# Attention's second pass, block by block: one two-bank score tile, one exponential, and both groups' value products side by side

## The chip, the cores and the metric

The kernel runs on one core of a Trainium2 chip. The metric is the device time of one execution in microseconds, the median of several. Before the change it is 3320.48 us, the median of 3 runs (3320.19 to 3322.39).

## The reference, cut to what matters

The kernel computes two networks one after the other: a first block of two layers (an mLSTM mixer, then sliding-window attention, each with a feed-forward part) and a second block of two layers, each of which sums attention, gated linear attention (GLA) and a gated unit (SGU). The change touches the three attentions: that of the sliding window, and one in each layer of the second block. The second block's, over 512 latent and 256 context tokens, with 8 query heads in 2 key/value groups of 4:

```python
def attend(q, k, v):
    s = jnp.einsum('btgrd,blgd->bgrtl', q, k, preferred_element_type=jnp.float32) * (ATTN_HEAD_DIM ** -0.5)
    p = jax.nn.softmax(s, axis=-1)
    return jnp.einsum('bgrtl,blgd->btgrd', p.astype(v.dtype), v)
```

In the first of these layers the context tokens attend as well, among themselves. The sliding window has 16 query heads in 4 groups; a chunk of 128 latent queries sees the 256 context keys and the latent keys at most 128 positions away, and the softmax has one more term, a sink:

```python
s_lat = jnp.where(valid, s_lat, -jnp.inf)
m = jnp.maximum(jnp.maximum(jnp.max(s_lat, -1), jnp.max(s_ctx, -1)), sink_g)
p_lat = jnp.exp(s_lat - m[..., None])
p_ctx = jnp.exp(s_ctx - m[..., None])
den = jnp.sum(p_lat, -1) + jnp.sum(p_ctx, -1) + jnp.exp(sink_g - m)
o = jnp.einsum("bhgqk,bkhd->bqhgd", p_lat, vb) + jnp.einsum("bhgqc,bchd->bqhgd", p_ctx, cv)
return o / jnp.moveaxis(den, 3, 1)[..., None]
```

## The kernel before, in words

Large products take every operand as a high and a low part and sum three matmuls (high by high, high by low, low by high). Their results go to PSUM tiles named "acc" (two banks of 512 float32 values a partition, `acc()` at line 351), in some stages to more banks. A weight tile is loaded ("raw"), its high part is made on ScalarE ("whi") and its low part on VectorE or GpSimd ("wlo").

An attention has two passes over the keys, both on chunks of 128 queries. First the projections give keys and queries token by token; `stack_k` (line 1003) and `stack_q` (line 992) split them and transpose them on TensorE (against "k_ident", line 298) into a PSUM tile "st", from which ScalarE and VectorE copy the pieces into the operands "kh", "kl", "q", "q2" (in the sliding window the high keys lie in tiles that the trace calls "uhc" and "ulc").

The first pass (`stats`, line 1029) puts the scores with queries on the partitions into tiles "s" (3 banks), takes the extreme of each row on VectorE and the sum of exponentials on ScalarE. `stats_end` (line 1070) turns both into the logarithm of the softmax's denominator, transposes it (again a tile "st") and stores it by DMA as two more rows of "q2". So the second pass needs no further normalisation.

The second pass (`attend`, line 1111) goes over the blocks of 128 keys, and within a block over the two groups. For each group it puts the scores of four heads, keys on the partitions, into one bank (two matmuls of 512 columns, a third for a masked block), takes the exponential on ScalarE into "pT" and multiplies with the values "vt", adding into "o" (one bank). Group 0 writes partitions 0 to 63 of "o" and group 1 partitions 64 to 127. This product is in plain float32, and the machine runs it as two instructions of 512 columns. The score tiles are the two banks "st"; in later chunks, and for the sliding window's second pair of groups, they alternate with the three banks "s" (`banks`).

In the sliding window (`swa`, line 1140) there are two pairs of groups and four chunks, so eight calls of `attend`, with 4, 5, 5 and 4 key blocks for the four chunks: 36 blocks. Beside each call the statistics of the next chunk and, in the first four, the projections of the second pair are written. The first pair's results go to DRAM ("yd") and come back at the end, the second pair's are split at once. In the second block (`b_attn`, line 1270) the first layer has six chunks (four with 6 blocks, two of context with 2): 28 blocks, and the second has four chunks of 6: 24 blocks. After the attention `fill()` writes the projections for GLA and gates, which have nothing to do with the attention.

PSUM in these stages: acc 2 banks, st 2, s 3, o 1, which makes all eight.

The order on each engine isn't the written order alone. A planner in the language's tile layer walks all instructions with its own estimate of durations, gives each engine the earliest written instruction that its estimate has ready, and writes that order down; tiles with the same name share their buffers, and it adds the waits. The chip then runs each engine's list in that order. This is why matmuls of `fill()` stand between those of `attend` in the trace.

Of the kernel before, what the change touches and what calls it, by code (L numbers as in the profile page):

```python
# [239 lines left out]
class Net:  # L240
# [751 lines left out]
    def stack_q(self, ph, pc, x, q, q2):  # L992

        hl = self.t(ph, [P, 4, 2, 64], "qhl", F32R, bufs=2)
        self.act(hl[:, :, 0, :], x, scale=-0.125)
        self.stt(hl[:, :, 1, :], x, -0.125, hl[:, :, 0, :].bitcast(F32), MULT, SUB)
        pt = self.t(pc, [P, 4, P], "st", bufs=2)
        for r in range(4):
            self.tr(pt[:, r, :], hl[:, r].bitcast(F32).rearrange("p a d -> p (a d)"))
        self.act(q, pt)  # L1000
        self.nc.vector.tensor_copy(q2, pt[0:64])

    def stack_k(self, ph, pc, x, g, his, los):

        hl = self.t(ph, [P, 3, g, 64], "khl", F32R, bufs=1)
        hd = hl[:, 0:2].rearrange("p a g d -> p (a g d)").rearrange("p (g a d) -> p g a d", a=2, d=64)
        self.act(hd, x.unsqueeze(2).to_broadcast([P, g, 2, 64]))
        self.tt(hl[:, 2], x, hd[:, :, 0].bitcast(F32), SUB)
        for o in range(0, g, 2):
            pt = self.t(pc, [P, 4, P], "st", bufs=2)  # L1010
            for r in range(2):
                self.tr(pt[:, r, :], hd[:, o + r].bitcast(F32).rearrange("p a d -> p (a d)"))
            self.tr(pt[:, 2, :], hl[:, 2, o:o + 2].bitcast(F32).rearrange("p g d -> p (g d)"))
            for r in range(2):
                self.nc.vector.tensor_copy(his[o + r], pt[:, r])
                self.act(los[o + r], pt[64 * r:64 * r + 64, 2])
# [53 lines left out]
    def stats_end(self, ph, pc, parts):  # L1070
# [31 lines left out]
        self.split(hv[:, :, :, 0], hv[:, :, :, 1], d)  # L1102
        pt = self.t(pc, [P, P], "st", bufs=2)
        self.tr(pt, hl.bitcast(F32))
# [5 lines left out]

    def attend(self, ph, pc, q, q2, kh, kl, blocks, vs, masks={}, banks=None):


        po = self.t(pc, [P, 4, P], "o", bufs=1)
        for b in blocks:
            w = slice(b * P, b * P + P)
            for g in range(2):
                tag, n = next(banks) if banks else ("st", 2)
                ps = self.t(pc, [P, 4, P], tag, bufs=n)
                self.mm(ps, kh[g][:, w], q[:, 4 * g:4 * g + 4], stop=False)  # L1120
                self.mm(ps, kl[g][0:66, w], q2[0:66, 4 * g:4 * g + 4], start=False, stop=b not in masks)
                if b in masks:
                    self.mm(ps, self.identb, masks[b].unsqueeze(1).to_broadcast([P, 4, P]), start=False)
                pT = self.t(ph, [P, 4, P], "pT", bufs=4)
                self.act(pT, ps, AF.Exp, scale=-1.0)
                self.mm(po[64 * g:64 * g + 64], vs(b, g), pT, start=b == blocks[0], stop=b == blocks[-1])
        return po

# [11 lines left out]
    def swa(self, u, yd):  # L1140
# [10 lines left out]
        with self.pool("sw") as ph, self.pool("sws", side="right") as pg, self.pool("swp", space=PSUM) as pc:  # L1151
# [42 lines left out]
            qs, wq, y = {}, {}, {}  # L1194
            banks = itertools.cycle([("st", 2), ("st", 2), ("s", 3)])

# [21 lines left out]
            def attend(gp, c):  # L1218
# [6 lines left out]
                if c < 3:  # L1225
                    masks[1 + hi] = mb[:, 0]
                po = self.attend(ph, pc, *qs[gp, c], *keys(gp), [0, 1] + list(range(2 + lo, 2 + hi)),
                                 lambda b, g: vt[:, b, 2 * gp + g, :], masks, banks if gp else None)
                if gp == 0:
                    o = self.scr().rearrange("p (r t) -> p r t", r=4)  # L1230
                    self.act(o, po)
                    nc.sync.dma_start(out=yd[:, :, cs], in_=o)
                else:
                    if not y:
                        y.update(self.new_u("l"))
                    self.split(y["l"][0][:, 4:8, cs], y["l"][1][:, 4:8, cs], po)

# [6 lines left out]
            for n in range(8):  # L1244
# [3 lines left out]
                for g in range(2 if n < 4 else 0):  # L1248
                    project(1, g, n)
            for c in range(4):  # L1250
                x = self.scr()
# [18 lines left out]
    def b_attn(self, u, l, yd, fill):  # L1270
# [5 lines left out]
        with self.pool("at") as ph, self.pool("ats", side="right") as pg, self.pool("atp", space=PSUM) as pc:  # L1276
# [79 lines left out]
            half = len(qch) // 2  # L1356
            banks = itertools.cycle([("st", 2), ("st", 2), ("s", 3)])
            stats(qch[:half])
            for j, c in enumerate(qch):
                if j == 0:  # L1360
                    stats(qch[half:])
                t = slice(c * P, (c + 1) * P)
                po = self.attend(ph, pc, *qs[c], kh, kl, list(range(6 if c < 4 else 2)), lambda b, g: vt[:, b, g, :],
                                 banks=banks if j >= 2 else None)
                self.stt(yf[:, :, t], po, 0.5, yf[:, :, t], MULT, MULT)
                nc.sync.dma_start(out=yd[:, :, t], in_=yf[:, :, t])
            fill()
# [389 lines left out]
    def run(self):  # L1757
        nc = self.nc
        self.nw, self.nsc, self.nth, self.bg = 4, 5, 0, None
        with self.pool("cp") as self.cp, self.pool("up") as self.up, self.pool("sc") as self.sc, \  # L1760
# [217 lines left out]
```

## Time and profile before

| what | value |
|---|---|
| median of 3 runs | 3320.48 us |
| profiled execution, its own time | 3330.69 us |
| profiled execution, span | 3328.9 us |
| instructions | 51048, of them 19813 matmuls |
| VectorE busy | 1775.5 us (53%) |
| ScalarE busy | 1313.9 us (39%) |
| GpSimd busy | 1000.4 us (30%) |
| DMA, mean | 108 GB/s |

The profile is of one execution, and its span begins with the first instruction and ends with the last. An engine is busy while it has an instruction in work. Matmuls overlap one another: a row's duration is longer than the distance to the next one's start, so their durations can't simply be added; distances between starts are what the engine's time is made of. PEld is the loading of weights, which runs beside the matmuls. A merged row of the timeline ("x2", "x4") is so many instructions of one form that follow one another, from the first start to the last end. In square brackets stands how long the engine was idle before it, and what ended that.

### The profile page before, as it was taken

Reading aid. Unit: us, or ns where it says so; the run is one execution under the profiler, and the core shown is the slowest. Engines: PE = TensorE matmul, PEld = TensorE weight load, DVE = VectorE, ACT = ScalarE, POOL = GpSimd, SP = SyncE. Lnnn points to the kernel's source line nnn. Section 1 sums busy time; section 2 is a strip of 40 time slices with the busy share of each in tenths; the row PEclk is TensorE's granted clock in tenths of the full one; section 3 lists DMA queues with packets and bytes.
Section 4 is the critical chain, followed back from the end, with each engine's and each line's share of the span. In section 5 each row is a group of like instructions: output and inputs, shape, how many; then the busy total and the mean of one; then the engine's idle time right before and its main releaser. Section 6 shows DMA issues by size and latency. Waiting matters only on the chain.

```text
span 3328.9 us, 51048 instructions
## 1 busy us (share of the span) xinstructions
PE 3223.1 (97%) x19813; PEld 2600.0 (78%) x19813; DVE 1775.5 (53%) x3397; ACT 1313.9 (39%) x2650; POOL 1000.4 (30%) x950
## 2 busy tenths in 40 slices
PE   8999999999999999999999999999999999999898
PEld 5778887887788964778889885688788889658788
DVE  4566569567814753431137530388624685138856
ACT  4334342222122565422235553444321456345443
POOL 0122134344342210255553000144413640013444
PEclk9999999999999999999999999999999999999899
DMA  6543215544411111132222221312354312233372
GB/s 231 174 149 97 102 59 172 172 167 155 150 64 63 58 33 33 53 131 95 96 88 93 75 68 57 118 55 85 128 177 127 133 61 81 87 113 93 102 244 82
DMA packets 151938, 359.54 MB, mean 108 GB/s; under 512 B 16304, under 2 KB 52944, under 8 KB 149648
## 3 DMA queue, kind: packets, MB, share of 16 engines
q1 hardware_dynamic: 151696, 356.27, 32.3%
q8 instruction: 156, 2.56, 0.3%
q14 instruction: 86, 0.70, 0.1%
HBM read 316.35 MB, written 39.71 MB: 107 GB/s over the span
## 4 chain that ended last, share of the span: by engine, by line
PE 84%; DVE 7%; issue 3%; DMA 2%; POOL 2%; ACT 1%; SPq 0%; ACTq 0%; DVEq 0%; POOLq 0%
PE acc L294 42%; PE accx L294 22%; PE o L294 5%; PE s L294 4%; PE st L294 3%; PE ada L294 2%; PE num L294 2%; DVE aacc L290 2%; POOL zl L278 1%; DMA k<-gqk 1%; PE st L298 1%; PE x L294 1%; DVE gqt L290 1%; DVE ggx L278 1%; PE sm L294 0%
## 5 line engine op out<-in xcount | busy, mean ns | idle before, releaser
L278 POOL TENSOR_TENSOR wlo<-raw,whi 128x1024 fp32r<-128x1024 f32 x152 | 384.3, 2530 | 1067.4 <-ACT whi L274 870.5
L274 ACT ACTIVATE whi<-raw 128x1024 fp32r<-128x1024 f32 (+1 forms) x339 | 355.7, 1052 | 585.3 <-PE acc L294 288.3
L294 PE MATMUL acc<-uhl,whi 128*128 128x512 f32 (+2 forms) x1208 | 467.9, 388 | 6.0 <-DVE sc L290 2.6
L294 PE MATMUL acc<-ull,whi 128*128 128x512 f32 (+2 forms) x1208 | 466.0, 386 | 0.0
L294 PE MATMUL acc<-uhl,wlo 128*128 128x512 f32 (+2 forms) x1208 | 465.3, 386 | 0.0
L278 DVE TENSOR_TENSOR wlo<-raw,whi 128x1024 fp32r<-128x1024 f32 (+1 forms) x187 | 241.9, 1297 | 238.3 <-ACT whi L274 227.5
L294 PEld LDWEIGHTS acc<-uhl,whi 128*128 128x128 f32 (+1 forms) x1208 | 228.2, 189 | 58.5 <-issue 3.3
L290 DVE SCALAR_TENSOR_TENSOR aacc<-araw,cond,aacc 128x512 f32<-128x512 f32 x266 | 268.0, 1050 | 5.3 <-DMA araw<-in_ws_dram 3.9
L294 PEld LDWEIGHTS acc<-uhl,wlo 128*128 128x128 f32 (+1 forms) x1208 | 227.9, 189 | 52.3 <-issue 6.9
L294 PEld LDWEIGHTS acc<-ull,whi 128*128 128x128 f32 (+1 forms) x1208 | 228.5, 189 | 45.9 <-issue 3.4
L294 PE MATMUL acc<-whi,ull 128*128 128x256 f32 x736 | 214.1, 292 | 3.6 <-DVE ull L290 3.5
L294 PE MATMUL acc<-whi,uhl 128*128 128x256 f32 x736 | 214.9, 293 | 2.4 <-ACT uhl L274 2.2
L294 PE MATMUL acc<-wlo,uhl 128*128 128x256 f32 x736 | 213.2, 290 | 0.7 <-DVE wlo L278 0.7
L294 PE MATMUL accx<-uhl,whi 128*128 128x512 f32 (+2 forms) x544 | 200.0, 369 | 6.3 <-ACT uhl L274 3.6
L278 DVE TENSOR_TENSOR al<-sc,ah 128x512 fp32r<-128x512 f32 (+1 forms) x99 | 76.0, 770 | 243.0 <-ACT ah L274 242.8
L294 PE MATMUL accx<-ull,whi 128*128 128x512 f32 (+2 forms) x544 | 200.1, 368 | 2.0 <-DVE ull L290 2.0
L294 PE MATMUL accx<-uhl,wlo 128*128 128x512 f32 (+2 forms) x544 | 199.0, 366 | 0.0
L1042 DVE TENSOR_REDUCE nm<-s 128x1 f32<-128x512 f32 (+2 forms) x184 | 118.8, 663 | 140.3 <-PE s L294 139.4
L294 PE MATMUL acc<-uhc,whi 128*128 128x256 f32 (+1 forms) x656 | 187.5, 286 | 1.6 <-ACT uhc L274 1.6
L294 PE MATMUL acc<-uhc,wlo 128*128 128x256 f32 (+1 forms) x656 | 188.0, 287 | 0.0
L294 PE MATMUL acc<-ulc,whi 128*128 128x256 f32 (+1 forms) x656 | 187.0, 285 | 0.0
L294 PE MATMUL o<-pT,vt 128*64 128x512 f32 x352 | 170.5, 616 | 0.9 <-ACT pT L274 0.7
(487 smaller groups left out, 7825.2 us busy)
## 6 DMA issues: line engine op xcount, KB each, us to landing
raw<-in_ws_dram SPq DMA_DIRECT2D x336, 512.0 KB
araw<-in_ws_dram SPq DMA_DIRECT2D x192, 256.0 KB
araw<-in_ws_dram SPq DMA_DIRECT2D x32, 512.0 KB
th<-sc SPq DMA_DIRECT2D x48, 256.0 KB
th<-th SPq DMA_DIRECT2D x24, 384.0 KB
ar<-in_ws_dram SPq DMA_DIRECT2D x8, 1024.0 KB
mb<-mcd SPq DMA_DIRECT2D x48, 128.0 KB
cb<-mcd SPq DMA_DIRECT2D x48, 128.0 KB
```

The costliest lines, as they stand in the source:

```text
L274: self.last = self.nc.scalar.activation(out, in_, f, **kw)
L278: r = (eng or self.nc.vector).tensor_tensor(out, a, b, op=op)
L290: self.lastv = self.nc.vector.scalar_tensor_tensor(out, a, s, b, op0=op0, op1=op1)
L294: self.nc.tensor.matmul(ps, l, r, start=start, stop=stop)
L298: self.nc.tensor.transpose(ps, x, self.ident[:k, :k])
L1042: nc.vector.tensor_reduce(nm[:, e, h:h + k], ps, axis=AX.X, op=MIN)
```

## The change

Only the second attention pass and the tiles around it change.

- The scores of both groups of a key block go to one tile "st2" of two banks, of which there is one. One exponential of 1024 values a partition reads it into one pT tile (two buffers instead of four of half the size).
- The two products with the values of a block are written one behind the other, and a block late: after the scores and the exponential of the next block, which may be that of the next chunk. `attend_end` writes the last one. What follows a chunk's last product (evacuating "o", the store to DRAM, the split) is a function `done` that is called then.
- The "s" banks aren't used for the second pass any more (`banks` is gone).
- The transposes of `stack_q`, `stack_k` and `stats_end` get their tiles from `acc()` instead of "st".

PSUM afterwards: acc 2 banks, st2 2, s 3, o 1.

```diff
--- before.py
+++ after.py
@@ -994,7 +994,7 @@
         hl = self.t(ph, [P, 4, 2, 64], "qhl", F32R, bufs=2)
         self.act(hl[:, :, 0, :], x, scale=-0.125)
         self.stt(hl[:, :, 1, :], x, -0.125, hl[:, :, 0, :].bitcast(F32), MULT, SUB)
-        pt = self.t(pc, [P, 4, P], "st", bufs=2)
+        pt = self.acc().rearrange("p (r t) -> p r t", r=4)
         for r in range(4):
             self.tr(pt[:, r, :], hl[:, r].bitcast(F32).rearrange("p a d -> p (a d)"))
         self.act(q, pt)
@@ -1007,7 +1007,7 @@
         self.act(hd, x.unsqueeze(2).to_broadcast([P, g, 2, 64]))
         self.tt(hl[:, 2], x, hd[:, :, 0].bitcast(F32), SUB)
         for o in range(0, g, 2):
-            pt = self.t(pc, [P, 4, P], "st", bufs=2)
+            pt = self.acc().rearrange("p (r t) -> p r t", r=4)
             for r in range(2):
                 self.tr(pt[:, r, :], hd[:, o + r].bitcast(F32).rearrange("p a d -> p (a d)"))
             self.tr(pt[:, 2, :], hl[:, 2, o:o + 2].bitcast(F32).rearrange("p g d -> p (g d)"))
@@ -1100,7 +1100,7 @@
         nc.gpsimd.memset(hl[:, 16 * n:].bitcast(F32), 0.0)
         hv = hl[:, :16 * n].rearrange("p (k h a) -> p k h a", k=n, a=2)
         self.split(hv[:, :, :, 0], hv[:, :, :, 1], d)
-        pt = self.t(pc, [P, P], "st", bufs=2)
+        pt = self.acc(P)
         self.tr(pt, hl.bitcast(F32))
         lt = self.t(ph, [16 * n, P], "lt", F32R, bufs=2)
         nc.vector.tensor_copy(lt, pt[:16 * n])
@@ -1108,23 +1108,38 @@
             for a in range(2):
                 nc.sync.dma_start(out=q2[64 + a:65 + a].bitcast(F32), in_=lt[16 * k + a:16 * k + 16:2].bitcast(F32))
 
-    def attend(self, ph, pc, q, q2, kh, kl, blocks, vs, masks={}, banks=None):
-
-
-        po = self.t(pc, [P, 4, P], "o", bufs=1)
+    def attend(self, ph, pc, q, q2, kh, kl, blocks, vs, done, masks={}):
+
+
+
+        po = None
         for b in blocks:
             w = slice(b * P, b * P + P)
+            ps = self.t(pc, [P, 2, 4, P], "st2", bufs=1)
             for g in range(2):
-                tag, n = next(banks) if banks else ("st", 2)
-                ps = self.t(pc, [P, 4, P], tag, bufs=n)
-                self.mm(ps, kh[g][:, w], q[:, 4 * g:4 * g + 4], stop=False)
-                self.mm(ps, kl[g][0:66, w], q2[0:66, 4 * g:4 * g + 4], start=False, stop=b not in masks)
+                self.mm(ps[:, g], kh[g][:, w], q[:, 4 * g:4 * g + 4], stop=False)
+                self.mm(ps[:, g], kl[g][0:66, w], q2[0:66, 4 * g:4 * g + 4], start=False, stop=b not in masks)
                 if b in masks:
-                    self.mm(ps, self.identb, masks[b].unsqueeze(1).to_broadcast([P, 4, P]), start=False)
-                pT = self.t(ph, [P, 4, P], "pT", bufs=4)
-                self.act(pT, ps, AF.Exp, scale=-1.0)
-                self.mm(po[64 * g:64 * g + 64], vs(b, g), pT, start=b == blocks[0], stop=b == blocks[-1])
-        return po
+                    self.mm(ps[:, g], self.identb, masks[b].unsqueeze(1).to_broadcast([P, 4, P]), start=False)
+            pT = self.t(ph, [P, 2, 4, P], "pT", bufs=2)
+            self.act(pT, ps, AF.Exp, scale=-1.0)
+            self.attend_end()
+
+            def values(b=b, pT=pT):
+                nonlocal po
+                if po is None:
+                    po = self.t(pc, [P, 4, P], "o", bufs=1)
+                for g in range(2):
+                    self.mm(po[64 * g:64 * g + 64], vs(b, g), pT[:, g], start=b == blocks[0], stop=b == blocks[-1])
+                if b == blocks[-1]:
+                    done(po)
+
+            self.values = values
+
+    def attend_end(self):
+        if self.values:
+            self.values()
+        self.values = None
 
     def rope(self, ph, x, cos, sin, swapped, out):
 
@@ -1192,7 +1207,6 @@
                     self.stack_k(ph, pc, kf[j], 4, [x[:, o] for x in kh], [kl[0:64, g, o] for g in range(4)])
             kl = [kl[:, g] for g in range(4)]
             qs, wq, y = {}, {}, {}
-            banks = itertools.cycle([("st", 2), ("st", 2), ("s", 3)])
 
             def project(gp, g, c):
                 if (gp, g) not in wq:
@@ -1224,16 +1238,19 @@
                     masks[2 + lo] = mb[:, 1]
                 if c < 3:
                     masks[1 + hi] = mb[:, 0]
-                po = self.attend(ph, pc, *qs[gp, c], *keys(gp), [0, 1] + list(range(2 + lo, 2 + hi)),
-                                 lambda b, g: vt[:, b, 2 * gp + g, :], masks, banks if gp else None)
-                if gp == 0:
-                    o = self.scr().rearrange("p (r t) -> p r t", r=4)
-                    self.act(o, po)
-                    nc.sync.dma_start(out=yd[:, :, cs], in_=o)
-                else:
-                    if not y:
-                        y.update(self.new_u("l"))
-                    self.split(y["l"][0][:, 4:8, cs], y["l"][1][:, 4:8, cs], po)
+
+                def done(po):
+                    if gp == 0:
+                        o = self.scr().rearrange("p (r t) -> p r t", r=4)
+                        self.act(o, po)
+                        nc.sync.dma_start(out=yd[:, :, cs], in_=o)
+                    else:
+                        if not y:
+                            y.update(self.new_u("l"))
+                        self.split(y["l"][0][:, 4:8, cs], y["l"][1][:, 4:8, cs], po)
+
+                self.attend(ph, pc, *qs[gp, c], *keys(gp), [0, 1] + list(range(2 + lo, 2 + hi)),
+                            lambda b, g: vt[:, b, 2 * gp + g, :], done, masks)
 
             for o in (0, 2):
                 for g in range(2):
@@ -1247,6 +1264,7 @@
                 attend(*divmod(n, 4))
                 for g in range(2 if n < 4 else 0):
                     project(1, g, n)
+            self.attend_end()
             for c in range(4):
                 x = self.scr()
                 nc.sync.dma_start(out=x, in_=yd[:, c])
@@ -1354,16 +1372,17 @@
 
             qch = sorted(qch)
             half = len(qch) // 2
-            banks = itertools.cycle([("st", 2), ("st", 2), ("s", 3)])
             stats(qch[:half])
             for j, c in enumerate(qch):
                 if j == 0:
                     stats(qch[half:])
-                t = slice(c * P, (c + 1) * P)
-                po = self.attend(ph, pc, *qs[c], kh, kl, list(range(6 if c < 4 else 2)), lambda b, g: vt[:, b, g, :],
-                                 banks=banks if j >= 2 else None)
-                self.stt(yf[:, :, t], po, 0.5, yf[:, :, t], MULT, MULT)
-                nc.sync.dma_start(out=yd[:, :, t], in_=yf[:, :, t])
+
+                def done(po, t=slice(c * P, (c + 1) * P)):
+                    self.stt(yf[:, :, t], po, 0.5, yf[:, :, t], MULT, MULT)
+                    nc.sync.dma_start(out=yd[:, :, t], in_=yf[:, :, t])
+
+                self.attend(ph, pc, *qs[c], kh, kl, list(range(6 if c < 4 else 2)), lambda b, g: vt[:, b, g, :], done)
+            self.attend_end()
             fill()
 
     def gla(self, u, l, dr, fill):
@@ -1756,7 +1775,7 @@
 
     def run(self):
         nc = self.nc
-        self.nw, self.nsc, self.nth, self.bg = 4, 5, 0, None
+        self.nw, self.nsc, self.nth, self.bg, self.values = 4, 5, 0, None, None
         with self.pool("cp") as self.cp, self.pool("up") as self.up, self.pool("sc") as self.sc, \
                 self.pool("xd", space=DRAM) as xd, self.pool("pa", space=PSUM) as self.pa:
             self.accs = [(self.pa, "acc", 2)] * 2
```

## Rows read from the trace of the kernel before

**Rows 1.** The page: TensorE's busy time; the chain by engine, by line.

```profile
PE 3223.1 (97%) x19813; PEld 2600.0 (78%) x19813; DVE 1775.5 (53%) x3397; ACT 1313.9 (39%) x2650; POOL 1000.4 (30%) x950
...
PE acc L294 42%; PE accx L294 22%; PE o L294 5%; PE s L294 4%; PE st L294 3%; PE ada L294 2%; PE num L294 2%; DVE aacc L290 2%; POOL zl L278 1%; DMA k<-gqk 1%; PE st L298 1%; PE x L294 1%; DVE gqt L290 1%; DVE ggx L278 1%; PE sm L294 0%
```

**Rows 2.** Stretches: length, busy PE, PEld, DVE, ACT, POOL, clock, DMA share, GB/s.

```profile
1090.00:1185.00 95.00, 95.00 (x797) 92.93 (x796) 68.78 (x173) 53.72 (x141) 19.01 (x21) 1.00 0.15 51
1185.00:1352.00 167.00, 161.49 (x646) 76.60 (x646) 58.35 (x144) 97.81 (x253) 7.81 (x13) 1.00 0.10 30
1940.00:2113.00 173.00, 173.00 (x781) 107.74 (x781) 24.23 (x43) 60.92 (x118) 6.68 (x3) 1.00 0.19 62
2840.00:2952.00 112.00, 112.00 (x379) 55.55 (x379) 9.76 (x17) 36.86 (x64) 7.62 (x6) 1.00 0.19 59
```

**Rows 3.** Timeline, end of the last attention: start, length, engine, line, operation, tiles.

```profile
2946.18 1.08 PE L294 MATMUL o<-pT,vt 128*64 128x512 f32 x4
...
2947.19 0.50 PE L294 MATMUL st<-q,kh 128*128 128x512 f32 x1
...
2947.53 0.39 PE L294 MATMUL st<-q,kl 66*128 66x512 f32 x1
...
2947.85 1.07 PE L294 MATMUL o<-pT,vt 128*64 128x512 f32 x2
2948.02 0.60 ACT L274 ACTIVATE pT<-st 128x512 f32<-128x512 f32 x1 [0.58 <-PE st L294]
...
2948.85 0.50 PE L294 MATMUL st<-q,kh 128*128 128x512 f32 x1
...
2949.51 2.38 PE L294 MATMUL o<-pT,vt 128*64 128x512 f32 x8
...
2950.17 0.59 ACT L274 ACTIVATE pT<-s 128x512 f32<-128x512 f32 x1
...
2950.81 0.19 PEld L294 LDWEIGHTS o<-pT,vt 128*64 128x64 f32 x2 [0.26 <-ACT pT L274]
```

**Rows 4.** Timeline, a little earlier: scores that follow one another.

```profile
2939.55 0.40 PE L294 MATMUL st<-q,kl 66*128 66x512 f32 x1
...
2939.78 0.40 PE L294 MATMUL st<-q,kh 128*128 128x512 f32 x1
```

**Rows 5.** Timeline: the first product with the values; one between other matmuls.

```profile
1187.44 1.07 PE L294 MATMUL o<-pT,vt 128*64 128x512 f32 x2
...
2050.08 1.07 PE L294 MATMUL o<-pT,vt 128*64 128x512 f32 x2
...
2051.08 0.50 PE L294 MATMUL st<-q,kh 128*128 128x512 f32 x1
```

**Rows 6.** Stretches, only instructions of "o": length, busy PE, PEld, DVE, ACT.

```profile
1185.00:1352.00 167.00, 71.64 (x144) 13.23 (x144) 2.76 (x4) 4.78 (x8) 1.00 0.10 30
1940.00:2113.00 173.00, 53.46 (x112) 9.94 (x112) 3.81 (x6) 0.00 (x0) 1.00 0.19 62
2830.00:2952.00 122.00, 45.41 (x96) 8.56 (x96) 2.16 (x4) 0.00 (x0) 1.00 0.21 68
```

**Rows 7.** ScalarE's groups by form: count, busy us, mean ns, idle before.

```profile
L274 ACT ACTIVATE whi<-raw 128x1024 fp32r<-128x1024 f32 x336 | 354.5, 1058 | 580.5 <-PE acc L294 288.1 <-PE accx L294 264.0 <-issue 24.1
L274 ACT ACTIVATE pT<-st 128x512 f32<-128x512 f32 x146 | 86.1, 597 | 203.5 <-PE st L294 202.3 <-PE o L294 0.9
```

**Rows 8.** Chain (one projection), timeline (a query tile's readers), tile "st" (its transposes).

```profile
1150.67 2.92 PE acc L294 x24
...
1138.33 0.60 ACT L274 ACTIVATE q<-st 128x512 fp32r<-128x512 f32 x1 [2.96 <-PE st L298]
...
1138.96 0.68 DVE L1001 CAST q<-st 64x512 fp32r<-64x512 f32 x1 [1.32 <-ACT q L274]
...
L298 PE MATMUL st<-k_ident,qhl x144: 270/272/329, 1137.7 to 2734.8; 128*128 128x128 f32 x144
...
L298 PE MATMUL st<-k_ident,khl x72: 270/272/474, 1107.6 to 2710.6; 128*128 128x128 f32 x72
```

## The prediction

> **What bounds the kernel now.** I read the page's busy line and chain first: TensorE is busy for 97% of the span, and the chain that ended last runs through matmuls almost only; the products with the values ("PE o") alone are 5% of it [rows 1]. Then I read the stretches in which the second attention pass runs. There are three: the sliding-window layer (1185 to 1352 us), and the attention of the two second-block layers (1940 to 2113 us and 2840 to 2952 us). In the second and third TensorE is busy in every microsecond, in the first for 161.5 of 167, always at full clock, 2.4 GHz; ScalarE is busy for 98 us of the first's 167, 61 of 173 and 37 of 112 [rows 2]. So TensorE's time is the kernel's time there, and the question is what the change does to that engine's time and which waits it brings. The end of the kernel itself isn't touched; time saved in these stages is saved at the end, since the chain passes through all three.
>
> "Busy" isn't "used well", and the timeline shows where it goes. Each product with the values is two instructions of 128 rows by 64 columns and 512 values. Alone, such a product holds TensorE for 1.00 us from its start to the next other matmul (2947.85 to 2948.85). Where the planner happened to put the products of both kv groups side by side, which write the two halves of the partitions, four instructions take 1.01 us together (2946.18 to 2947.19) [rows 3]: the two halves of the array work at once. In the filled stages a lone product costs the same 1.00 us (2050.08 to 2051.08) [rows 5].
>
> Going in and out costs too. Scores that follow one another start 0.23 us apart [rows 4]. From the last score matmul to a product it is 0.32 us (2947.53 to 2947.85), and the first matmul after a product keeps the next one off for 0.34 us (2947.19 to 2947.53) [rows 3]. So each run of products pays 0.09 + 0.11 = 0.20 us beside its own time.
>
> **The change part by part.**
>
> *Both values' products adjacent.* There are 88 key blocks (36 in the sliding-window layer, 28 and 24 in the two others), so 176 products of two instructions: 144 + 112 + 96 = 352 [rows 6]. Following TensorE's instructions in order they stand in 152 separate runs (64, 48 and 40; the first at 1187.44, the last at 2949.51) [rows 5, 3]; 139 of these are a single product. The products' busy time is 71.6 + 53.5 + 45.4 = 170.5 us [rows 6]; each run's end overlaps the next matmul's start by 0.07 us (1.07 long, 1.00 to the next), so they hold the engine for 170.5 - 152 x 0.07 = 159.9 us. After the change both products of a block wait for one and the same exponential and stand next to each other, so there are 88 runs of 1.01 us: 88.9 us. That saves 71.0 us. 64 runs fewer save 64 x 0.20 = 12.8 us. Together 83.8 us: 36.4 in the sliding-window layer, 25.8 and 21.6 in the two others, by the same working on each stage's row. If two blocks meet in a run it is a little more; I don't count it.
>
> *One exponential for both groups.* 176 exponentials of 0.60 us [rows 7] become 88 of 1024 values a partition. None of that size out of PSUM is in the trace; it lies between the 1.06 us of a 128x1024 copy on ScalarE out of SBUF [rows 7] and two of today's, 1.20. I take 1.06, the row with the same length. ScalarE gains 88 x 0.14 = 12 us, worth nothing by itself, as ScalarE is not the bound.
>
> *One two-bank tile instead of two to five score tiles.* This is the new wait. The scores of a block can't start before the exponential of the block before has read the tile. Where nothing fills, a block's round is: three score matmuls at 0.23, the fourth's 0.39, 0.1 until the exponential starts (2947.53 + 0.39 to 2948.02), 1.06, and 0.05 to 0.2 until TensorE goes on (2950.17 + 0.59 to 2950.81 is 0.05) [rows 3]: 2.3 to 2.45 us. TensorE's own work in it is 4 x 0.23 + 1.01 + 0.20 = 2.13. The product a block late lies beside the exponential and hides most of it; what is left is 0.15 to 0.3 us a block. It is nil where other matmuls (next chunk's statistics, projections of the fill) stand between, as in most of 1940 to 2113. Bounds: 0 to 88 x 0.3 = 26; I take 0.2 on the some 30 blocks with no filling (the end of the last stage, where 14 blocks run bare, and the end of the first): 6 us.
>
> In the sliding-window layer the exponential also queues on ScalarE behind those of the next chunk's statistics. TensorE's part there falls from 161.5 to some 125 us while ScalarE keeps 98 - 36 x 0.14 = 93: three quarters busy, in order, with one score tile. I take 8 us of new waits (bounds 0 and 25, about 0.2 and 0.7 a block).
>
> *Transposes moved to the two "acc" banks.* 36 query tiles (144 transposes), 24 key tiles (72) and 12 of the statistics, 72 in all [rows 8], leave the "st" pair and share "acc" with the projections. A query tile is held for 1.31 us by its two readers (1138.33 to 1138.96 + 0.68), a projection fills its own bank for 2.9 us (24 matmuls) [rows 8]. With two banks for both, the next projection may have to wait for one. Where the fill and the scores stand ready it costs nothing. Bounds: 0 and 72 x 0.6 = 43 (half the hold each time); I take 0.1 a tile, 8 us, nearer to nothing because a tile's hold is less than half of the projection that can run beside it.
>
> *A block late.* It changes the order, not the work: the evacuation of "o" and its store (14 on SP's queue) come one block later, and the next thing due is that the following chunk's first product needs "o" back. One block's scores stand between now, 0.92 us against an evacuation of 0.6 to 0.7 [rows 6], so I cost it at nothing; without that cover it is 18 chunks x 0.7 = 13 us, in the range. The pT buffers are of the same size as before.
>
> Sum: -83.8 + 6 + 8 + 8 = -62 us, on the profiled execution's 3330.69 us, which is 1.8 above its span and 10.2 above the median. By the median: 3320.5 - 62 = 3258.
>
> The Trainium skill, "TensorEngine Tiling (Array Packing)", section Performance Considerations, warns that tiling speeds up the multiplications but not the reading of PSUM, which may become the bound. By this rule the gain would stop where ScalarE's reading does; the trace has ScalarE busy for 33 to 59% of these stages [rows 2], so it bears the rule out at most in the first. It is the third case below.
>
> **The rivals.**
> 1. *All of it arrives.* The planner finds filling for each wait, and the acc banks never collide: -84, 3236 us. For it: TensorE is never short of work in 1940 to 2113 now. Against: 14 blocks at the end of the last stage run bare, with no work to fill with.
> 2. *The exponential becomes the bound.* One score tile and one queue: each block waits some 0.5 us (0.2 bare, and half of another 0.6 us exponential ahead in the queue): 44 + 8 for the banks, so -84 + 52 = -32, 3288 us. For it: all four scores must end before the exponential starts, and nothing else is buffered. Against: ScalarE is far from full in the last two stages.
> 3. *Slower: the two acc banks.* Each of the 72 transposed tiles keeps TensorE from its next projection for its whole hold, 1.31 us: 94 us, with the other 14 that is +24, 3344 us. It decides from (84 - 14) / 72 = 0.97 us a tile. For it: in the query and key phases projections and transposes alternate, and two banks must carry both. Against: a tile's hold is under half of the 2.9 us for which the other bank keeps TensorE at a projection, and in the attention stages scores are there to run.
> 4. *The change doesn't do what it says*: the planner orders by its own clock and puts other matmuls between the two products, so that they run one after another as now: 152 runs or more, 3320 us. Against: both become ready at the same instant and are written one after the other.
>
> **How the numbers follow.** Chances: forecast 0.62, rival 1 0.14, rival 2 0.14, rival 3 0.06, rival 4 0.04. 0.2% is 6.6 us, about what a measurement can tell from no change. Faster: 0.62 + 0.14 + 0.14 = 0.90; same 0.04; slower 0.06. The forecast's own range, from its costs' bounds, is 3240 to 3278; the 80% range takes in rivals 1 and 2 with a margin of some 6 us: 3230 to 3294.
>
> **What would show it.** In the profile after: 88 or fewer runs of "o" with four instructions in 1.0 to 1.1 us, and the products' busy time near 95 us in place of 170.5; 88 exponentials of about 1.06 us into pT; the three stages shorter by some 26, 23 and 17 us. Wrong would be: "o" still in pairs of two instructions; TensorE waiting on "ACT pT" for more than some 20 us in all; or TensorE waiting on the readers of "acc" in the query and key phases (1090 to 1185 us and those before the two other stages) for tens of microseconds; in 1090 to 1185 it is now busy throughout [rows 2].

## The result, and the profile after

The changed kernel takes 3516.7 us (median of 4, 3511.4 to 3525.0) against 3321.4 beside it: 1.059 times the time before, 95% interval 1.0568 to 1.0611. The forecast was 62 us faster; it became 195 us slower. The profiled execution has a span of 3509.6 us, 180.7 more than before, and all rows below are of profiled executions.

Three stretches tell where it went. Each begins with the first key transposes of an attention; the first ends with the last product of the sliding window, the two others where GLA's first matmuls begin. First the kernel before (length, then busy time of TensorE, weight load, VectorE, ScalarE and GpSimd with their instructions, granted clock, DMA share, GB/s):

```profile
1107.60:1349.50 241.90, 237.08 (x1283) 150.67 (x1281) 113.04 (x279) 140.09 (x370) 23.83 (x30) 1.00 0.11 36
1786.40:2117.80 331.40, 331.40 (x1854) 254.00 (x1851) 121.75 (x269) 153.69 (x367) 34.66 (x35) 1.00 0.20 64
2687.50:2957.00 269.50, 269.46 (x1368) 197.67 (x1368) 103.38 (x215) 129.66 (x295) 27.93 (x28) 0.99 0.24 78
```

The same stretches of the kernel after:

```profile
1104.20:1359.30 255.10, 223.69 (x1314) 161.24 (x1312) 114.75 (x281) 135.11 (x334) 23.11 (x30) 0.93 0.10 34
1788.40:2212.30 423.90, 358.47 (x1916) 288.38 (x1916) 123.87 (x269) 152.57 (x340) 30.30 (x34) 0.88 0.18 59
2787.10:3131.30 344.20, 293.23 (x1453) 228.31 (x1453) 103.42 (x219) 129.66 (x277) 25.88 (x29) 0.87 0.22 70
```

They are 13.2, 92.5 and 74.7 us longer, together 180.4 of the 180.7. TensorE, which was idle for 5 us in them, is idle for 1023.2 - 875.4 = 148 us. And its busy time is 37 us longer although the products became cheaper. Two things are in that: 178 more matmuls fall into the stretches (4683 against 4505, mostly projections that the kernel before had issued ahead of the first key transposes), and the granted clock fell from 0.99 to 1.00 down to a mean of 0.87 to 0.93.

The products themselves did what was forecast. Of "o" alone, after (columns as in [rows 6]):

```profile
1185.00:1362.00 177.00, 38.85 (x144) 7.13 (x144) 2.74 (x4) 4.77 (x8) 0.99 0.13 43
2000.00:2140.00 140.00, 31.48 (x112) 5.75 (x112) 3.52 (x6) 0.00 (x0) 0.96 0.18 59
2955.00:3081.00 126.00, 26.80 (x96) 4.86 (x96) 2.76 (x4) 0.00 (x0) 0.97 0.19 65
```

They take 97.1 us instead of 170.5, in 87 runs instead of 152. The exponential too (ScalarE's group: count, busy us, mean ns, idle before):

```profile
L274 ACT ACTIVATE pT<-st 128x1024 f32<-128x1024 f32 x88 | 90.0, 1023 | 145.1 <-PE st L294 144.7
```

What TensorE waited for, longest first, in the whole kernel after (us in total, times, longest):

```profile
PE acc L298 <- DVE qhl L290: 71.1, 16, 7.2
PE acc L298 <- ACT khl L274: 31.3, 8, 12.1
PE s L294 <- ACT s L274: 28.5, 31, 3.8
PE s L298 <- ACT khl L274: 24.0, 7, 8.5
```

Line 298 is the transposes. They wait 71 + 31 + 24 = 126 us for their own operands, the split queries and keys. (The 24 us are of tiles named "s": in the key phase of the second block `acc()` hands out the three banks "s" as well, line 1329, so there five banks served projections and transposes, and they waited all the same.) In the kernel before, that kind of wait came to one of 5.4 us:

```profile
PE st L298 <- ACT khl L274: 5.4, 1, 5.4
```

One round of the query phase, in the timeline of the kernel after, shows how a transpose comes to wait:

```profile
1885.16 0.41 PE L294 MATMUL acc<-whi,ulc 128*128 128x256 f32 x1
1885.37 0.41 PE L294 MATMUL acc<-wlo,uhc 128*128 128x256 f32 x1
...
1888.05 0.28 PE L294 MATMUL acc<-whi,uhc 128*128 128x256 f32 x1
...
1888.29 0.28 PE L294 MATMUL acc<-wlo,uhc 128*128 128x256 f32 x1
1888.60 0.38 ACT L274 ACTIVATE sc<-acc 128x256 f32<-128x256 f32 x1 [4.11 <-PE acc L294]
...
1889.79 1.02 POOL L278 TENSOR_TENSOR nms<-nms,nhalf 128x4 f32<-128x4 f32 x1 [8.06 <-DVE nms L287]
...
1891.81 0.42 ACT L274 ACTIVATE qhl<-no 128x256 fp32r<-128x256 f32 x1 [2.55 <-DVE no L278]
1892.26 0.42 DVE L290 SCALAR_TENSOR_TENSOR qhl<-no,qhl 128x256 fp32r<-128x256 f32 x1 [0.54 <-ACT qhl L274]
1892.84 1.09 PE L298 MATMUL acc<-k_ident,qhl 128*128 128x128 f32 x4 [4.27 <-DVE qhl L290]
1893.58 0.56 PE L294 MATMUL acc<-whi,uhc 128*128 128x256 f32 x1
```

A projection ends at 1888.29; its result goes through ScalarE (1888.60), VectorE, GpSimd (1889.79) and ScalarE again (1891.81), and TensorE stands idle for 4.27 us until its four transposes can start at 1892.84. Only behind them comes the next projection, at 1893.58. The projection that ends at 1888.29 had begun behind such a wait too, and most of it runs slowly: its matmuls start 0.21 us apart (1885.16, 1885.37) at a granted clock of 0.50, and only its last ones 0.12 apart (two within 0.24, 1888.05 to 1888.29). The stretch in which it is slow:

```profile
1883.60:1887.50 3.90, 3.90 (x20) 3.90 (x19) 0.68 (x1) 0.60 (x1) 0.00 (x0) 0.50 0.00 0
```

The order of TensorE's instructions says the same. In the first of the second block's layers there are 18 projections of 24 matmuls, 6 for the keys and then 12 for the queries. Counted in the two traces, so many had been issued when the transposes of a query tile began:

| query tile | 1 | 2 | 3 | 4 | 5 | 6 | 7 | 8 |
|---|---|---|---|---|---|---|---|---|
| before | 10.7 | 11.9 | 12.0 | 14.1 | 14.5 | 15.8 | 15.9 | 17.0 |
| after | 7 | 8 | 9 | 10 | 11 | 12 | 13 | 14 |

Before, projections run some three to four chunks further ahead of the transposes. After, they alternate strictly in the written order.

### The profile page after: what moved, and what is told of

It is laid out like the page before. It is cut to its first block, busy times and chain, and to the rows that moved or that the text cites. A ratio compares the mean times of both kernels' runs of the same rounds, so it can differ in the third digit from the quotient of the medians.

```text
span 3509.6 us, 50898 instructions
## 1 busy us (share of the span) xinstructions
PE 3235.2 (92%) x19813; PEld 2652.7 (76%) x19813; DVE 1774.4 (51%) x3397; ACT 1306.0 (37%) x2562; POOL 987.6 (28%) x950
## 4 chain that ended last, share of the span: by engine, by line
PE 78%; DVE 11%; ACT 4%; issue 3%; POOL 3%; DMA 1%; SPq 0%; ACTq 0%; POOLq 0%; DVEq 0%
PE acc L294 42%; PE accx L294 21%; PE s L294 3%; PE st L294 3%; PE o L294 2%; PE ada L294 2%; PE num L294 2%; DVE aacc L290 2%; PE acc L298 1%; DVE gqt L290 1%; POOL zl L278 1%; POOL nms L278 1%; DVE nm L1042 1%; ACT s L274 1%; DVE gst L290 1%
## 5 line engine op out<-in xcount | busy, mean ns | idle before, releaser
L294 PE MATMUL acc<-whi,uhl 128*128 128x256 f32 x728 | 232.2, 319 | 6.3 <-ACT kl L274 4.9
L294 PE MATMUL acc<-whi,ull 128*128 128x256 f32 x728 | 228.5, 314 | 4.6 <-DVE ull L290 4.5
L294 PE MATMUL acc<-wlo,uhl 128*128 128x256 f32 x728 | 226.0, 311 | 0.0
L274 ACT ACTIVATE sc<-acc 128x512 f32<-128x512 f32 (+2 forms) x213 | 102.4, 482 | 206.2 <-PE acc L294 162.3
L294 PEld LDWEIGHTS acc<-whi,ull 128*128 128x128 f32 x728 | 160.0, 220 | 16.7 <-issue 10.5
```

The lines of the kernel that those rows point to most:

```text
L274: self.last = self.nc.scalar.activation(out, in_, f, **kw)
L294: self.nc.tensor.matmul(ps, l, r, start=start, stop=stop)
```

## The experiments

Theory A: the loss is the shared "acc" ring, and the rest of the change does what was forecast. Rival B: the loss is the single two-bank score tile and the late order. The first four kernels tell them apart from both sides.

**Only the transposes moved**, in the kernel before:

```diff
-        pt = self.t(pc, [P, 4, P], "st", bufs=2)
+        pt = self.acc().rearrange("p (r t) -> p r t", r=4)
```

(in `stack_q` and `stack_k`, and likewise in `stats_end`.)

> The kernel before with one edit: the transposes of stack_q, stack_k and stats_end take their PSUM tile from acc() instead of "st"; the second attention pass is the old one. Theory A (the loss is the shared acc ring: each transpose stands in the ring between two projections, so TensorE waits for the whole chain from a projection to its transposes): the query and key phases grow as in the changed kernel (some 49 us before the second attention's first product, some 20 before the third's, and fill pushed behind the attention), and there are no paired products to pay for it: 3320 + 195 + 60 to 84 = 3575 to 3600 us. Rival B (the single two-bank score tile and the late order make the loss, the acc banks cost 20 us at most): 3325 to 3345 us.

It took 3578.5 us, 1.0762 times the kernel before (1.0734 to 1.0790): 251 us, as theory A had it. Its waits are those of the changed kernel almost to the microsecond:

```profile
PE acc L298 <- DVE qhl L290: 71.1, 17, 7.2
PE acc L298 <- ACT khl L274: 29.8, 8, 12.2
PE s L294 <- ACT s L274: 27.2, 33, 2.6
PE s L298 <- ACT khl L274: 22.4, 6, 8.5
```

**The changed kernel with the transposes elsewhere**, in three places: the score tile, a bank of their own, the ring of the statistics.

```diff
-        pt = self.acc().rearrange("p (r t) -> p r t", r=4)
+        pt = self.t(pc, [P, 4, P], "st2", bufs=1)     # score tile
+        pt = self.t(pc, [P, 4, P], "st", bufs=1)      # own bank, "s" with 2 buffers
+        pt = self.t(pc, [P, 4, P], "s", bufs=3)       # the statistics' ring
```

> The changed kernel with one edit: the transposes take their tile from "st2", the single two-bank tile of the scores, and acc() serves projections alone again. Theory A: projections run ahead of the transposes again, TensorE's waits for qhl and khl go away, and the paired products pay: 3240 to 3290 us (in the sliding window the second pair's query transposes now stand in one ring with the scores, which may cost 10 to 20 us of it). Rival B: the score tile is still single, so nearly all of the loss stays: 3470 to 3520 us.

> The changed kernel with the transposes in a bank of their own ("st", one buffer), taken from the statistics' "s" (2 banks instead of 3). Theory A: 3240 to 3275 us, less whatever the statistics lose with two banks (up to 15). Rival B: 3470 to 3520 us.

> The changed kernel with the transposes in the ring "s" of three banks that the statistics use. In the second block the statistics are written behind all query transposes, so there is nothing to stand in line for; in the sliding window the second pair's transposes alternate with the statistics. Theory A: 3235 to 3280 us. Rival B: 3470 to 3520 us.

Measured: 3279.9 us (ratio 0.9861, 0.9843 to 0.9878), 3276.3 (0.9856, 0.9830 to 0.9882) and 3303.8 (0.9934, 0.9913 to 0.9955). One and the same change is 5.9% slower or 1.4% faster by where the transposes' tile comes from; B falls. The first is inside its range; the two others come out 1 and 24 us above theirs, so some 33 us of the forecast 84 were still missing in the best (51 us faster).

**Written order or too few banks?** The changed kernel, transposes still in the two acc banks, but written behind the next chunk's projection:

```diff
                 ps = self.acc(256)
                 self.tmm(ps, self.uchunk(u, c), wq)
+                self.flush()                  # the chunk before: stack_q
                 x = normed(...)
-                self.stack_q(ph, pc, x, ...)
+                self.late.append(lambda x=x, ...: self.stack_q(ph, pc, x, ...))
```

(`stack_k` likewise.)

> The changed kernel, transposes still in the two acc banks, but stack_q and stack_k are written one chunk later, behind the next chunk's projection. Theory A1 (the ring hands its tiles out in written order, so a projection can't be issued before the transposes written ahead of it, and those wait for the chain ScalarE, VectorE, GpSimd behind their own projection): now the chain lies beside the next projection, the wait per tile falls from some 4.5 us to 1.5 to 2, and most of the loss goes: 3320 to 3400 us. Rival A2 (two banks are too few for projections and transposes, in whatever order they are written): 3480 to 3530 us, as the changed kernel.

It took 3380.4 us, 1.0170 times (1.0149 to 1.0190): with the same banks 136 us of the loss go, of some 240 that lie between the changed kernel and the one with an own bank. The waits on the queries:

```profile
PE acc L298 <- DVE qhl L290: 9.5, 9, 2.3
```

So more than half of the loss was the order, and A2 falls as the main cause. What is left, 104 us above the kernel with an own bank, may have both in it; no run separates them.

**Which tiles?** On the best kernel found (below, 3233 us), only the 36 query tiles moved to acc.

> The kernel with the products ordered together (3233 us) with one edit: only the 36 query tiles of stack_q go to acc(), the key tiles and the statistics' stay in "st". Theory A1 (the price is TensorE standing at a query's transposes for the chain behind its projection): the waits on qhl were 71 of some 126 us, so about 56% of the 251 us that all 72 tiles cost the kernel before: 3350 to 3400 us. Rival (the key tiles, of which two follow each projection, or the statistics' tiles carry most of it): 3250 to 3300 us.

3416.3 us, 1.0271 times the kernel before (1.0242 to 1.0301): 183 us above the kernel without the edit, 5.1 a tile. The queries carry most of it, and the time is 16 us above the range that I had reckoned from the waits, which are 65 us:

```profile
PE acc L298 <- DVE qhl L290: 65.3, 18, 7.2
```

So a microsecond of this wait cost nearly three. The two profiled executions say where: TensorE is idle for 214 us instead of 100, with 25 us of waits of the statistics' scores among it (2 without the edit), and busy for 66 us more (3199.1 against 3133.1), at a granted clock of 0.964 instead of 0.986 in the mean.

**Where is the missing part of the gain?** First the pairing alone: two score banks and an exponential for each group as before, transposes in "st", products written next to each other and a block late.

```diff
+            pT = self.t(ph, [P, 2, 4, P], "pT", bufs=2)
             for g in range(2):
+                ps = self.t(pc, [P, 4, P], "st", bufs=2)
                 ... scores of group g into ps ...
+                self.act(pT[:, g], ps, AF.Exp, scale=-1.0)
```

> Only the pairing: "st" stays two buffers of one bank, which the transposes use as before, each group has its own exponential, and the two products of a block stand next to each other a block late. Theory A (the paired products pay some 84 us of TensorE less the new waits; the loss of the changed kernel is the acc ring alone): query and key phases as before, 3240 to 3270 us. Rival C (the gain needs the single exponential or the two-bank tile as well, or the missing part of the 84 us in the last two kernels is lost in the attention itself): 3270 to 3320 us, no better than the 3276 to 3280 of the kernels with the transposes moved out of acc.

3318.7 us, ratio 0.9983 (0.9973 to 0.9992): next to nothing, outside theory A's range and at the end of C's. Its timeline shows why, in a stretch without filling:

```profile
2919.79 0.50 PE L294 MATMUL st<-q,kh 128*128 128x512 f32 x1
2920.13 0.39 PE L294 MATMUL st<-q,kl 66*128 66x512 f32 x1
2920.45 1.07 PE L294 MATMUL o<-pT,vt 128*64 128x512 f32 x2
...
2921.45 0.50 PE L294 MATMUL st<-q,kh 128*128 128x512 f32 x1
```

Each product still stands alone between scores, in 157 runs. Each becomes ready with its own exponential, and the planner issues it then, whatever stands next to it in the source. In the kernels with one score tile and one exponential for both groups they stand in 85 to 90 runs. That the common exponential does it, and not the common tile, is argued: no run has the one without the other.

Then the same kernel with the order prescribed:

```diff
+            self.lasts = self.lastp            # the block's last score matmul
...
+                with self.tc.issue_after(self.lasts.ins):
                     for g in range(2):
                         self.mm(po[64 * g:64 * g + 64], vs(b, g), pT[:, g], ...)
```

> The pairing-only kernel (two score banks, an exponential for each group, transposes in "st"), with one edit: both products of a block are ordered on TensorE behind the next block's last score matmul, so that the planner can't issue the first as soon as its own exponential is done. In the order that results they stand in 85 runs (157 without the edit). Theory P (the pairing-only kernel gained nothing because its products did not come to stand together; standing together is what pays): 3250 to 3280 us. Rival Q (what pays in the repaired kernels is the single exponential and the fewer, larger score tiles, not the products side by side): 3305 to 3325 us, as without the edit.

3233.1 us, ratio 0.9725 (0.9703 to 0.9746): 93 us faster than before, the best of all, and below its range. The timeline is now one run of four instructions a block:

```profile
2836.58 0.50 PE L294 MATMUL st<-q,kh 128*128 128x512 f32 x1
2836.92 0.40 PE L294 MATMUL st<-q,kl 66*128 66x512 f32 x1
2837.16 0.40 PE L294 MATMUL st<-q,kh 128*128 128x512 f32 x1
2837.40 0.40 PE L294 MATMUL st<-q,kl 66*128 66x512 f32 x1
2837.42 1.08 ACT L274 ACTIVATE pT<-st 128x512 f32<-128x512 f32 x2 [1.06 <-PE st L294]
2837.73 1.08 PE L294 MATMUL o<-pT,vt 128*64 128x512 f32 x4
2838.74 0.50 PE L294 MATMUL st<-q,kh 128*128 128x512 f32 x1
```

From one block's first score to the next block's it is 2.16 us (2836.58 to 2838.74), with no gap: 4 x 0.23 + 1.01 + 0.20 = 2.13 had been reckoned for TensorE alone. Group 0's exponential lies beside group 1's scores, so its bank is free again in time; the round of 2.3 to 2.45 us that I had reckoned for a single two-bank tile isn't there. In the changed kernel with an own bank for the transposes it is, 2.37 us from block to block:

```profile
2880.11 0.50 PE L294 MATMUL st<-q,kh 128*128 128x512 f32 x1 [0.16 <-ACT pT L274]
...
2881.24 1.08 PE L294 MATMUL o<-pT,vt 128*64 128x512 f32 x4
2882.48 0.50 PE L294 MATMUL st<-q,kh 128*128 128x512 f32 x1 [0.17 <-ACT pT L274]
```

The three stretches of the ordered kernel:

```profile
1102.60:1310.10 207.50, 204.35 (x1283) 145.72 (x1281) 112.05 (x279) 136.64 (x370) 23.68 (x30) 0.98 0.14 42
1746.90:2052.50 305.60, 305.60 (x1855) 248.86 (x1853) 121.37 (x269) 152.64 (x367) 35.15 (x35) 1.00 0.22 72
2614.60:2862.00 247.40, 247.38 (x1369) 194.23 (x1369) 103.25 (x215) 129.44 (x295) 27.94 (x28) 0.99 0.27 85
```

They are 34.4, 25.8 and 22.1 us shorter than before. The same of the changed kernel with an own bank for the transposes:

```profile
1103.40:1335.20 231.80, 212.86 (x1282) 149.79 (x1281) 115.75 (x279) 137.70 (x334) 19.71 (x30) 0.96 0.12 37
1770.90:2085.20 314.30, 311.05 (x1859) 252.05 (x1859) 123.15 (x267) 151.58 (x338) 30.42 (x34) 0.99 0.22 70
2648.00:2900.60 252.60, 250.78 (x1373) 195.47 (x1373) 102.83 (x216) 128.53 (x271) 26.12 (x28) 0.99 0.27 83
```

So its missing part lies in the sliding window above all: 24 us, with 19 us of TensorE idle and a clock of 0.96.

Three more kernels looked for a better place. Query and key transposes before an attention in "s", those within it in "st2":

> The changed kernel with the transposes that come before an attention in the ring "s" (three banks, idle then), and those within an attention (the second pair's queries of the sliding window, and the statistics' logarithms) in "st2". Theory A: the key and query phases as short as in the kernel with all transposes in "s", the attentions as short as in the one with all in "st2": 3255 to 3275 us. If what is missing of the gain is lost in the attention (single score tile), not before it: 3275 to 3300 us.

3299.7 us (0.9928, 0.9910 to 0.9946). Theory A missed, and the time lies at the end of the other range, though not for its reason: the two second-block stretches grew again to 324 and 267 us, and what is lost there is lost before the attention. I had taken "s" for idle there. But in the second block's key phase `acc()` hands out the banks "s" as well, so the key transposes again shared a ring with projections, and waited for their keys (in the two stretches):

```profile
PE s L298 <- ACT khl L274: 6.7, 4, 3.0
PE s L298 <- ACT khl L274: 8.1, 4, 3.9
```

The kernel with all transposes in "s" (3303.8 us) has 15.4 us of the same wait. Two banks for the transposes that are given back before the score tile needs them:

> The changed kernel with the transposes before an attention in two banks "st" that are given back before the score tile "st2" takes them; within the sliding window's attention the transposes have a bank of their own (the statistics keep two). Theory A: the key and query phases as in the kernel before (242 us from the first key transpose to the sliding window's last product there, 331 and 270 us from the first key transposes to GLA's start in the two layers), the attentions as in the kernel with an own bank: 3255 to 3272 us. If the acc ring's harm is all that the other repaired kernels still carry, it can't be better than those: 3270 to 3285 us.

3263.1 us (0.9814, 0.9799 to 0.9829): some 13 us better than the own bank, the best with the single two-bank tile. And the ordered kernel with the old alternation between "st" and "s":

> The same with the score tiles alternating between "st" and the statistics' "s" as in the kernel before (second pair of the sliding window, later chunks of the second block). Theory P with waits for a score tile as what is missing: 5 to 15 us better than the kernel without it. If score tiles are not what is missing: within 5 us of it.

3264.0 us (0.9817, 0.9800 to 0.9833), 31 us worse than without, which neither range had: more score tiles didn't help. In its order 16 products stand alone again; that explains only part of the 31 us, and the rest stays open.

## Why the prediction was wrong, point by point

- **Both values' products adjacent: right.** 97.1 us of products against some 95 forecast, 87 runs against 88. That it is worth -83.8 us (36.4, 25.8, 21.6) is shown by the pair of kernels that differ in nothing but whether the products stand together: 3318.7 and 3233.1 us, 85.6 apart. Stage by stage the pair differs by 32.1, 27.3 and 23.9 us; the stages of the one with the products apart:

```profile
1104.40:1344.00 239.60, 237.34 (x1282) 148.84 (x1281) 112.07 (x279) 138.67 (x370) 23.59 (x30) 1.00 0.11 36
1779.80:2112.70 332.90, 332.77 (x1853) 250.68 (x1852) 121.19 (x267) 154.93 (x367) 34.48 (x34) 1.00 0.20 66
2673.10:2944.40 271.30, 271.25 (x1367) 196.65 (x1367) 103.38 (x215) 131.21 (x295) 27.93 (x28) 0.99 0.24 77
```

- **One exponential: right in size** (1023 ns against 1060), and probably with a use that I hadn't seen: it makes both products ready at once. I had put down the planner's separating them as a rival with a chance of 0.04, because they would "become ready at the same instant"; with two exponentials they don't, and it does.
- **One two-bank tile: right where blocks run bare, open beyond that.** I had 6 + 8 us, with bounds of 0 to 26 and 0 to 25. Bare blocks are 2.37 us apart where 2.3 to 2.45 had been reckoned, and the scores' waits for the exponential come to 3.5 us in the changed kernel and to this in the one with an own bank:

```profile
PE st L294 <- ACT pT L274: 6.2, 25, 1.3
```

  With that own bank the three stretches are 10.1 + 17.1 + 16.9 = 44 us shorter than before, in the ordered kernel 82. The 38 us between them include the smaller rings for transposes and statistics; the 13 us between the own bank and the two banks given in turn are of that kind. The other 25 or so are left for the tile and all else that differs, by subtraction and not measured alone; the 6.2 us of waits are a quarter of them.
- **A block late: nothing, as I had costed it.** The kernel with the late order and the products still apart takes 3318.7 us, 0.9983 times the kernel before: no cost shows.
- **Transposes moved to the "acc" banks: the step that failed.** I took "0.1 a tile, 8 us", with bounds of 0 and 43. Moving the 72 tiles alone cost 251 us, 3.5 a tile. (The forecast's range, 3240 to 3278, was narrower than the costs' bounds that it was said to come from: with 26 + 25 + 43 + 13 us it would have reached 3344, and the result lies beyond that too.) Two things were wrong. I priced how long a tile is held by its readers (1.31 us), but what counts is how long TensorE waits for its writers (the sign of being wrong that I had named looked at the readers of "acc" as well): tiles of one ring are issued in the order in which they are written, so a transpose that isn't ready keeps the next projection from TensorE, and the wait is the whole chain from a projection to its own transposes, 4.27 us in the round above, less what may be issued from other rings. And I took the fill and the scores as cover: but the fill takes its tiles from the same ring, and scores need these very queries. The Trainium skill, "TensorE: Matmul & The Clock Gate", section Part 3, says that matmuls start and end in program order; the rows agree, as nothing passes the transposes at 1892.84. That is why a wait at the head of TensorE's list costs all that stands behind it.
- **The rival of the acc banks (3344 us) had the place and the sign**, with a chance of 0.06 and a price of 1.31 us a tile; it decided, but at 3.5. What would have shown it before: [rows 8] have the readers of a tile, while the chain ahead of it, POOL's 1.02 us among its pieces, was in the trace and wasn't followed.
- **The clock.** I had taken full clock for granted. In a stretch in which TensorE stood and went by turns it was granted 0.73 in the mean:

```profile
1850.00:1950.00 100.00, 63.04 (x313) 55.35 (x311) 43.13 (x94) 38.78 (x107) 12.45 (x14) 0.73 0.05 15
```

  so a wait was paid twice, once as idle time and once in the projection behind it (0.21 instead of 0.12 us a matmul). Over the whole execution, with the same 19813 matmuls, TensorE's idle time grew by 169 us (3509.6 - 3235.2 = 274.4 against 3328.9 - 3223.1 = 105.8). Its busy time grew by 12 us where 84 less were due, so by subtraction some 96 us go with the slower clock, 0.952 in the mean against 0.984. The Trainium skill, same page, section Part 1, has the throttled clock as the default that activity lifts; the rows agree in direction.

## What to carry to other kernels

Before moving a tile to another ring, write down the order in which that ring's tiles are written, and ask for each whether its writer's operands are ready when its turn comes: the price is the chain ahead of the tile, not the time for which it is held. Work that should stand together on an engine has to become ready together or be ordered explicitly; standing together in the source isn't enough where a planner orders. And where a change has one part with a sure gain and others that only make room for it, price the room with as much care, and leave that part as it was if it can be left: the kernel that keeps the old tiles and only orders the products is 93 us faster than before, the full change 195 slower.

## What the runs showed of the hardware

- Products of 64 columns into the two halves of the partitions run at once where they stand next to each other; at the full clock four take 1.08 us as two take 1.07, in every kernel here. They needn't come from the same exponential or score tile.
- An exponential of 128x1024 out of two PSUM banks takes 1023 ns, against 2 x 597 for two of one bank.
- With TensorE idle for over a third of a stretch, in pieces of up to 7.2 us, its granted clock was 0.73 in the mean, of the two levels 1.2 and 2.4 GHz; in the kernel before, never idle in that stage, 1.00.
